# Fetching the attention projection's results as whole tiles, with the conv taps spaced two per cent closer

## The chip, the cores and the metric

The kernel runs on one core of one Trainium2 chip. The metric is the device time of one execution in microseconds, as the median of several runs. The engines are PE (TensorE matmul; PEld its weight load), DVE (VectorE), ACT (ScalarE), POOL (GpSimd) and SP (SyncE), whose queue issues this kernel's DMAs in order.

## The reference: a block with a convolution branch and an attention branch

For x of 2048 tokens by 1024 channels, in float32, the reference computes (cut to what matters)

```python
h = rmsnorm(x, norm_g)
glu_in, cgate, q, k, v, agate, merge = split(h @ w_in)         # 7680 columns
conv = conformer_conv(glu_in)     # a * sigmoid(b); 31-tap causal depthwise conv; layernorm; silu
yc = (conv * silu(cgate)) @ w_conv_out
attn = sliding_window_attention(rope(q), rope(k), v, sinks)    # 16 heads, 4 kv heads, window 128
ya = (attn * silu(agate)) @ w_attn_out
merged = sigmoid(m_c) * yc + sigmoid(m_a) * ya
out = rmsnorm(x + merged @ w_out, final_norm_g)
```

In the kernel's names ma and mc are the two merge gates, before their sigmoid, and mp is the result of the attention projection, ya.

## The kernel before, in words

**Tiling.** Two sweeps s of T = 1024 tokens; each sweep is two halves of TH = 512. Channels are tiles of 128 (KC = 8). Activations lie channels first, so a projection of one channel tile e over one half is 8 chunks of the contraction into one PSUM bank of 128x512. Each product is made of three matmuls on a high and a low part of both operands (`product`), so a half takes 24 matmuls and an item, both halves of one e, 48. `load_w` fetches an item's weights as two raw tiles of 256 KB (L266), casts the high part on ACT (L282) and, in sweep 0, subtracts the low part (L262) and stores it; in sweep 1 the low part is fetched again (L284). Weights have four buffers of each kind and are prefetched one item ahead, `early` the raw part another item ahead.

**Stages of a sweep.** First the projections of the normalised input by w_in, with the attention (scores sc, L808 to L885) worked in between them. Then the 8 items of ya, whose evacuation copies the bank (L1052) and stores it to DRAM as d_mp (L1053). Then the 8 items of yc. Then the output stage o: 16 blocks of 128 tokens by 512 columns, 24 matmuls each (L1204), whose weights wo are fetched (L1147), cast (L1149) and split (L262), into the slots C0 to C7. In ya's time the background work prepares uT, the gated convolution result that yc multiplies.

**The evacuation of yc (`yc_item`, inner function `ev`).** For each half: fetch the gates ma and mc from DRAM (`load_gate`, DMA L599) and take their sigmoids on ACT (L600), fetch mp's half (L1078); on DVE multiply mp by its gate (L1079), multiply the PSUM bank by the other gate (L1080), which frees the bank; add the two on POOL (L1081); cast to the high part of mT on ACT (L343) and subtract the low part on DVE (L262). mT is what the output stage multiplies by. The profile calls the tiles lma, lmc and lmp.

**Buffers.** `t2k` is a ring of five tiles of 128x512 for such short-lived data (L86): gates on their way in and out, squares, and in yc lma, lmc and lmp. `mm_ps` has three PSUM banks for all big projections. `slot` hands out tiles of 128x1024 by tag; a slot that is taken again waits for the last reader of what was in it. The tags C0 to C7 hold the convolution's results cv until uT is made, and later wo; X0 and X2 hold layernorm's mean and the attention's values, both done before yc; C6, C7 and A14 hold GLU blocks in turn, so that the GLU block 7 waits for the last tap on block 5.

**What sets the order.** PE's order is written out by a planner (`Line`): it counts matmul time and, for background work, lets one operation go out after every so many microseconds (`line.every`; CONV_EVERY for the 31 taps of each channel tile's convolution, L532 for the first and L539 for the others, on DVE), while attention steps go out as chains by due time (ATT_EVERY 13.8 us). Evacuations are issued with raised priority. The other engines' rows are ordered by a scheduler. `od` stamps an operation so that stamped operations keep the order in which they were written.

Of the kernel before, what the change touches and what calls it, by code (L numbers as in the profile page):

```python
# [12 lines left out]
F32 = mybir.dt.float32  # L13
# [3 lines left out]
ALU = mybir.AluOpType  # L17
AX = mybir.AxisListType

P = 128  # L20
S = 2048
D = 1024
KC = D // P
T = 1024
NSWEEP = S // T
NB = T // P
TH = 512
# [16 lines left out]
LN_SUB = 2.6  # L44
GLU_AFTER = (0, 6, 12, 16, 19, 22, 25, 28)
ROPE_EVERY = 3.2
CONV_EVERY = 2.5
ATT_EVERY = 13.8
LAT = (19.0, 18.5)
SCORE_GAP = 3.2  # L50
# [6 lines left out]
def hybrid_block(ctx: ExitStack, tc: tile.TileContext, x, xt, par_d, w_in, w_conv, sinks, w_attn, w_out,  # L57
                 fin_g, rope_t, out):
    nc = tc.nc
    pe, act, dve, pool = nc.tensor, nc.scalar, nc.vector, nc.gpsimd  # L60
# [19 lines left out]
    C = [f"c{i}" for i in range(8)]  # L80
    X = [f"x{i}" for i in range(3)]
    WIDE = {"c6", "c7", "a14"}

    def slot(tag, shape, dt, name):
        n = int(np.prod(shape[1:]))
        full = 1024 + P if tag in WIDE else 1024  # L86
        t = slots.tile([P, full], dt, tag=tag, name=name)
        v = t[:, 0:n]
        if len(shape) == 3:
            v = v.rearrange("p (a b) -> p a b", b=shape[2])  # L90
        elif len(shape) == 4:
            v = v.rearrange("p (a b c) -> p a b c", b=shape[2], c=shape[3])
        return v

    def t2k(name, dt=F32):
        return work.tile([P, TH], dt, tag="t2k", name=name, bufs=5)
# [68 lines left out]
    d_mp = dram.tile([NSWEEP * KC, P, T], F32, name="d_mp")  # L165
# [85 lines left out]
    def od(op):  # L251

        tc.stamp_issue_order_token(op.ins, "chain")
        return op
# [9 lines left out]
    def fetch_raw(src, name, kh):  # L264
        raw = stage.tile([P, 4, P], F32, tag="raw", name=f"raw_{name}{kh}")
        od(nc.sync.dma_start(out=raw, in_=src[:, 4 * kh:4 * kh + 4, :]))  # L266
        return raw

    def load_w(src, name, home=None, steps=None, raws=None):

        parts = []
        at = lo_at.setdefault((src.tensor.name, src.offset), len(lo_at))

        def part(kh):
            if home is None:
                raw = raws[kh] if raws else fetch_raw(src, name, kh)
                hi = stage.tile([P, 4, P], F32R, tag="whi", name=f"whi_{name}{kh}")
                lo = stage.tile([P, 4, P], F32R, tag="wlo", name=f"wlo_{name}{kh}")
            else:
                raw, hi, lo = (home[i][:, kh] for i in range(3))  # L280
                od(nc.sync.dma_start(out=raw, in_=src[:, 4 * kh:4 * kh + 4, :]))
            act.copy(hi, raw)  # L282
            if (at, kh) in lo_stored:
                od(nc.sync.dma_start(out=f(lo), in_=d_lo[at, kh]))  # L284
            else:
                split_lo(lo, raw, hi, dve if steps is not None else pool)
            parts.append((hi, lo))

        for kh in range(2):
            if steps is None:  # L290
                part(kh)
            else:
                steps.append(lambda kh=kh: part(kh))

        def keep(kh):
            if (at, kh) not in lo_stored:
                lo_stored.add((at, kh))
                nc.sync.dma_start(out=d_lo[at, kh], in_=f(parts[kh][1]))

        return lambda k: (parts[k // 4][0][:, k % 4, :], parts[k // 4][1][:, k % 4, :]), keep  # L300

    def product(ps, w, r, k, order=(0, 1, 2)):
        parts = ((w[0], r[:, 0, :]), (w[0], r[:, 1, :]), (w[1], r[:, 0, :]))
        for i, (a, b) in enumerate(parts[n] for n in order):
            pe.matmul(out=ps, lhsT=a, rhs=b, start=(k == 0 and i == 0), stop=(k == KC - 1 and i == 2))  # L305

    def small_bank(name):
        return tp_ps.tile([P, 4, P], F32, tag="tp", name=name).rearrange("p a b -> p (a b)")

    def project(src, rhs, name, evac, halves=(0, 1), small=False):  # L310

        got = {}

        def early():
            got["raws"] = [fetch_raw(src, name, kh) for kh in range(2)]

        def prefetch():
            got["w"] = load_w(src, name, raws=got.get("raws"))

        prefetch.early = early  # L320

        def blocks():
            for half in halves:
                if small:
                    ps = small_bank(f"mm_{name}{half}")
                else:
                    ps = mm_ps.tile([P, TH], F32, tag="mm", name=f"mm_{name}{half}")
                for k in range(KC):
                    product(ps, got["w"][0](k), rhs(k, half), k)
                    if k == KC - 1:  # L330
                        with tc.high_priority(offset=PRIO):
                            evac(half, ps)
                    if half == halves[-1] and k % 4 == 3:
                        got["w"][1](k // 4)
                    yield 3 * MM_US

        return prefetch, blocks, (src, name, evac)
# [4 lines left out]
    def put_split(dst, src32, lo_eng):  # L342
        act.copy(dst[:, 0, :], src32)  # L343
        split_lo(dst[:, 1, :], src32, dst[:, 0, :], lo_eng)

    def make_tiles(tags, half, name):
        return [slot(tags[half * 8 + k], [P, 2, TH], F32R, f"{name}{half}_{k}") for k in range(KC)]
# [164 lines left out]
    def program():  # L512
        for s in range(NSWEEP):
            yield from sweep(s)

    def sweep(s):
# [80 lines left out]
        def load_gate(kind, func, e, half):  # L597
            g = t2k(f"l{kind}{s}_{e}_{half}")
            nc.sync.dma_start(out=g, in_=spill[kind][s * KC + e, :, half * TH:(half + 1) * TH])  # L599
            act.activation(out=g, in_=g, func=func)  # L600
            return g
# [293 lines left out]
        def start_attention():  # L895
            line.after(10.0, prepare_attention(), lambda: True)
            for n in range(NKV * NB):
                line.after(22.0 + n * ATT_EVERY, attention(n),
                           lambda n=n: (n > 0 or 0 in qk or 0 in begun) and (n not in soft or ("ag", 2 * (n // NB) + 1) in stored))
            line.every = CONV_EVERY  # L900
            start_tail()
# [75 lines left out]
        aT, uT = [[None] * KC, [None] * KC], []  # L977
# [27 lines left out]
        def start_tail():  # L1005
            line.late.append((line.t, a_chain(), lambda: NKV * NB - 1 in done))
# [61 lines left out]


        mT = []  # L1070

        def yc_item(e):
            def ev(half, ps):
                if not mT:
                    mT.extend(make_tiles(AT, h, f"mT{s}_") for h in range(2))
                ga, g = (load_gate(kind, AF.Sigmoid, e, half) for kind in ("ma", "mc"))
                m = t2k(f"lmp{s}_{e}_{half}")
                nc.sync.dma_start(out=m, in_=d_mp[s * KC + e, :, half * TH:(half + 1) * TH])  # L1078
                dve.tensor_tensor(out=ga, in0=m, in1=ga, op=ALU.mult)  # L1079
                dve.tensor_tensor(out=g, in0=ps, in1=g, op=ALU.mult)  # L1080
                pool.tensor_tensor(out=g, in0=g, in1=ga, op=ALU.add)  # L1081
                put_split(mT[half][e], g, dve)

            return project(w_conv[e], lambda k, half: uT[half][k], f"yc{s}_{e}", ev)

        def linked(item, after):
            def prefetch():
# [3 lines left out]
            return prefetch, item[1]  # L1091

        flat += [ya_item(e, e == 0) for e in range(KC)] + [yc_item(e) for e in range(KC)]
        for item, after in zip(flat, flat[1:]):
            yield linked(item, after)
# [186 lines left out]
```

## Time and profile before

| | |
|---|---|
| median of 3 runs | 2012.25 us (2010.91 to 2016.99) |
| the profiled execution, its own time | 2014.66 us |
| its span | 2013.0 us |
| its mean granted TensorE clock | 0.995 |
| bytes moved | 402.92 MB, mean 200 GB/s |

The span is the stretch from the first to the last recorded instruction; the profiled execution's own time is 1.66 us longer than its span and 2.41 us over the median. All times of the trace are microseconds from the span's start. A row of the waits tells which instruction waited for which, for how long in all, how often, and the longest. In a row of the timeline the figures at the front are start and duration, and the bracket at the end is the engine's idle time before it, with what ended it. For yc, sweep 0 spans 816.20 to 916.58 and sweep 1 1818.00 to 1911.04; ya stands ahead of it, o behind.

### The profile page before, as it was taken

To read this page: it belongs to the slowest core of one execution; us is meant where nothing else is said; L and a number is where in the kernel's file an instruction comes from. 1 tells how busy PE (TensorE), PEld (TensorE's weight loads), DVE (VectorE), ACT (ScalarE), POOL (GpSimd) and SP (SyncE) were. 2 spreads that over 40 slices of the span, in tenths; PEclk is the share of its full clock that TensorE was granted. 3 is DMA by queue.
4 is the path that set the end of the run, shared out by engine and by line. 5 is a ranking of instruction groups with operands and counts; after the bars stand their busy time and mean duration, and the time that the engine had idled before them with its cause. 6 is when DMAs were issued, how large, how long until landed. Compare 5 with 4: busy or idle time off the path is not lost. (4 is left out here: it accounts for less than half of the span.)

```text
span 2013.0 us, 26940 instructions
## 1 busy us (share of the span) xinstructions
PE 1975.2 (98%) x9000; PEld 1637.7 (81%) x9000; DVE 1375.4 (68%) x1937; ACT 1019.6 (51%) x2396; POOL 430.2 (21%) x462
## 2 busy tenths in 40 slices
PE   8999999999999999989999999999999999999998
PEld 6888888888888888867888888888887888888777
DVE  6997688888888646343858657888887875452324
ACT  7322567556555346434623126776655554473322
POOL 0445333333333232341001121111111110001200
PEclk9999999999999999999999999999999999999999
DMA  8557755655666855757546575656565678466632
GB/s 305 189 186 225 240 171 185 198 184 185 193 199 209 283 163 184 234 196 259 209 136 241 167 235 174 188 184 193 187 188 181 211 223 263 156 235 209 224 132 84
DMA packets 296763, 402.92 MB, mean 200 GB/s; under 512 B 23984, under 2 KB 139056, under 8 KB 296624
## 3 DMA queue, kind: packets, MB, share of 16 engines
q1 hardware_dynamic: 296624, 401.20, 61.0%
q8 instruction: 71, 1.16, 0.2%
q14 instruction: 68, 0.56, 0.1%
HBM read 260.59 MB, written 140.51 MB: 199 GB/s over the span
## 5 line engine op out<-in xcount | busy, mean ns | idle before, releaser
L539 DVE SCALAR_TENSOR_TENSOR acc<-glu,par,acc 128x1024 f32<-128x1024 f32 x464 | 595.4, 1283 | 5.1
L1204 PE MATMUL o<-wo,mT 128*128 128x512 f32 x768 | 181.2, 397 | 9.5 <-ACT wo L1149 6.6
L1204 PEld LDWEIGHTS o<-wo,mT 128*128 128x128 f32 x768 | 146.4, 191 | 43.9 <-ACT wo L1149 7.9
L305 PE MATMUL mm_yc<-uT,whi_yc 128*128 128x512 f32 x512 | 160.6, 395 | 12.4 <-DVE lmc L1080 12.4
L305 PE MATMUL mm_cg<-hT,whi_cg 128*128 128x512 f32 x512 | 159.8, 393 | 0.0
L305 PE MATMUL mm_ma<-hT,whi_ma 128*128 128x512 f32 x512 | 159.6, 393 | 0.0
L305 PE MATMUL mm_ag<-hT,whi_ag 128*128 128x512 f32 x512 | 159.4, 392 | 0.0
L305 PE MATMUL mm_mc<-hT,whi_mc 128*128 128x512 f32 x512 | 158.3, 390 | 0.0
L305 PE MATMUL mm_ya<-aT,whi_ya 128*128 128x512 f32 x512 | 157.7, 389 | 0.0
L305 PE MATMUL mm_ga<-hT,whi_ga 128*128 128x512 f32 x448 | 139.5, 392 | 2.2 <-ACT glu L562 2.2
L305 PE MATMUL mm_gb<-hT,whi_gb 128*128 128x512 f32 x448 | 139.2, 392 | 0.0
L851 POOL TENSOR_SCALAR_AFFINE_SELECT pc<-pt 64x512 fp32r<-64x512 f32 x128 | 83.8, 654 | 250.2 <-ACT pt L846 225.8
L305 PEld LDWEIGHTS mm_yc<-uT,whi_yc 128*128 128x128 f32 x512 | 97.2, 191 | 35.0 <-issue 12.8
L872 DVE TENSOR_TENSOR ss<-ov,ss 64x256 f32<-64x256 f32 x128 | 54.0, 422 | 101.5 <-ACT ss L869 94.4
L305 PEld LDWEIGHTS mm_ya<-aT,whi_ya 128*128 128x128 f32 x512 | 96.1, 188 | 20.0
L305 PEld LDWEIGHTS mm_mc<-hT,whi_mc 128*128 128x128 f32 x512 | 95.2, 188 | 18.9
L305 PEld LDWEIGHTS mm_ag<-hT,whi_ag 128*128 128x128 f32 x512 | 94.4, 188 | 17.0
L305 PEld LDWEIGHTS mm_ma<-hT,whi_ma 128*128 128x128 f32 x512 | 94.3, 188 | 16.9
L305 PEld LDWEIGHTS mm_cg<-hT,whi_cg 128*128 128x128 f32 x512 | 94.0, 188 | 16.7
L818 DVE TENSOR_TENSOR ss<-sc,ss 128x192 f32<-128x192 f32 (+2 forms) x256 | 77.7, 345 | 38.8 <-ACT ss L815 37.3
L826 ACT ACTIVATE ss<-ss,st 128x129 f32<-128x129 f32 x256 | 100.0, 394 | 5.9 <-DVE st L823 5.6
L1079 DVE TENSOR_TENSOR lma<-lmp,lma 128x512 f32<-128x512 f32 x32 | 24.4, 763 | 114.5 <-DMA lmp<-d_mp 69.6
(452 smaller groups left out, 4428.9 us busy)
## 6 DMA issues: line engine op xcount, KB each, us to landing
qk<-d_q SPq DMA_DIRECT2D x64, 256.0 KB, 4.3
d_a<-ss SPq DMA_DIRECT2D x64, 256.0 KB, 3.6
aT<-d_a SPq DMA_DIRECT2D x32, 512.0 KB, 6.1
qk<-d_k SPq DMA_DIRECT2D x60, 256.0 KB, 4.5
d_k<-hlk SPq DMA_DIRECT2D x16, 512.0 KB, 4.7
d_q<-hq_c SPq DMA_DIRECT2D x16, 512.0 KB, 4.7
raw_ag<-in_w_in_dram SPq DMA_DIRECT2D x32, 256.0 KB, 4.7
d_ag<-ag SPq DMA_DIRECT2D x32, 256.0 KB, 2.8
```

The lines of the kernel that those rows point to most:

```text
L305: pe.matmul(out=ps, lhsT=a, rhs=b, start=(k == 0 and i == 0), stop=(k == KC - 1 and i == 2))
L539: od(dve.scalar_tensor_tensor(out=to, in0=glu[c][:, j:j + T], scalar=tap(c, j), in1=acc[c], op0=ALU.mult, op1=ALU.add))
L818: od(dve.tensor_tensor(out=part, in0=sc[:, 0, c0:3 * HD], in1=part, op=ALU.add))
L826: od(act.activation(out=ext[:, h, :], in_=ext[:, h, :], func=AF.Exp, bias=ngm[:, h:h + 1], accum_out=den[:, h:h + 1]))
L851: pool.affine_select(out=pc[at], in_=f(pt[0:HD, a]), pattern=[[0, 2 * GQ], [1, HD]], compare_op=ALU.is_ge, fill=0.0, base=0, channel_multi ...
L872: od(dve.tensor_tensor(out=to[r], in0=ovp[rows[r][0], :, r], in1=to[r], op=ALU.add))
L1079: dve.tensor_tensor(out=ga, in0=m, in1=ga, op=ALU.mult)
L1204: pe.matmul(out=ps, lhsT=a[:, c0:c0 + P], rhs=r, start=(k == 0 and i == 0), stop=(k == KC - 1 and i == 2))
```

## The change

The fetch of mp leaves the evacuation. An item's prefetch, which runs one item ahead of its matmuls, now also takes a slot of 128x1024, fetches both halves of mp into it by one DMA of 512 KB, and stamps that DMA so that it keeps its place among the weights' fetches. The slots are X2 and X0 for the first two items and C0 to C5 for the other six. The evacuation reads its half of that tile. The number of taps and of every other operation stays; the taps go out every 2.45 us of planned time in place of 2.5.

```diff
-CONV_EVERY = 2.5
+CONV_EVERY = 2.45
...
         mT = []
+        mp = {}
+        mp_tags = [X[2], X[0]] + C[0:6]
 
         def yc_item(e):
             def ev(half, ps):
...
                 ga, g = (load_gate(kind, AF.Sigmoid, e, half) for kind in ("ma", "mc"))
-                m = t2k(f"lmp{s}_{e}_{half}")
-                nc.sync.dma_start(out=m, in_=d_mp[s * KC + e, :, half * TH:(half + 1) * TH])
-                dve.tensor_tensor(out=ga, in0=m, in1=ga, op=ALU.mult)
+                dve.tensor_tensor(out=ga, in0=mp[e][:, half * TH:(half + 1) * TH], in1=ga, op=ALU.mult)
...
-            return project(w_conv[e], lambda k, half: uT[half][k], f"yc{s}_{e}", ev)
+            prefetch, blocks, _ = project(w_conv[e], lambda k, half: uT[half][k], f"yc{s}_{e}", ev)
+
+            def with_mp():
+                prefetch()
+                mp[e] = slot(mp_tags[e], [P, T], F32, f"mp{s}_{e}")
+                od(nc.sync.dma_start(out=mp[e], in_=d_mp[s * KC + e]))
+
+            with_mp.early = prefetch.early
+            return with_mp, blocks
```

Three places of the rows' order are needed below. In the names, the first figure behind lma, lmc, lmp or mm_yc is e and the second the half, so lma_5_0 is half 10 of the stage and lma_5_1 half 11 (both counted from 0); mT_0_4 is the tile of half 8 and mT_1_4 that of half 9. The last number of a name only tells tiles apart.

The first piece is SP's queue amid yc of sweep 1. Before:

```order
L599 DMA lma_4_0_16956<-d_ma 128x512
L599 DMA lmc_4_0_16959<-d_mc 128x512
L1078 DMA lmp_4_0_16962<-d_mp 128x512
L284 DMA wlo_yc_50_16920<-d_lo 128x512
L284 DMA wlo_yc_51_16924<-d_lo 128x512
L599 DMA lma_4_1_16994<-d_ma 128x512
L266 DMA raw_yc_60_16927<-in_w_conv_out_dram 128x512
L599 DMA lmc_4_1_16997<-d_mc 128x512
L266 DMA raw_yc_61_16929<-in_w_conv_out_dram 128x512
L1078 DMA lmp_4_1_17000<-d_mp 128x512
L599 DMA lma_5_0_17044<-d_ma 128x512
```

The same place after:

```order
L599 DMA lma_4_0_16936<-d_ma 128x512
L599 DMA lmc_4_0_16939<-d_mc 128x512
L599 DMA lma_4_1_16972<-d_ma 128x512
L284 DMA wlo_yc_50_16898<-d_lo 128x512
L284 DMA wlo_yc_51_16902<-d_lo 128x512
L1089 DMA mp_5_16905<-d_mp 128x1024
L599 DMA lmc_4_1_16975<-d_mc 128x512
L266 DMA raw_yc_60_16907<-in_w_conv_out_dram 128x512
L266 DMA raw_yc_61_16909<-in_w_conv_out_dram 128x512
L599 DMA lma_5_0_17022<-d_ma 128x512
```

The two fetches of lmp are gone, one fetch of mp for the next item stands behind that item's low weight parts, and the gate lma_4_1 has moved ahead of them.

The second piece is DVE at the same place. Before:

```order
L1079 TENSOR_TENSOR lma_4_1_16994<-lmp_4_1_17000,lma_4_1_16994 128x512
L262 TENSOR_TENSOR mT_0_4_16592<-lmc_4_0_16959,mT_0_4_16592 128x512
L1079 TENSOR_TENSOR lma_5_0_17044<-lmp_5_0_17050,lma_5_0_17044 128x512
L1080 TENSOR_TENSOR lmc_4_1_16997<-mm_yc_41_16969,lmc_4_1_16997 128x512
L262 TENSOR_TENSOR mT_1_4_16600<-lmc_4_1_16997,mT_1_4_16600 128x512
L1080 TENSOR_TENSOR lmc_5_0_17047<-mm_yc_50_17019,lmc_5_0_17047 128x512
L1079 TENSOR_TENSOR lma_5_1_17082<-lmp_5_1_17088,lma_5_1_17082 128x512
```

After:

```order
L1080 TENSOR_TENSOR lmc_4_0_16939<-mm_yc_40_16911,lmc_4_0_16939 128x512
L262 TENSOR_TENSOR mT_0_4_16580<-lmc_4_0_16939,mT_0_4_16580 128x512
L1079 TENSOR_TENSOR lma_5_0_17022<-mp_5_16905,lma_5_0_17022 128x512
L1080 TENSOR_TENSOR lmc_4_1_16975<-mm_yc_41_16947,lmc_4_1_16975 128x512
L1079 TENSOR_TENSOR lma_5_1_17058<-mp_5_16905,lma_5_1_17058 128x512
L262 TENSOR_TENSOR mT_1_4_16588<-lmc_4_1_16975,mT_1_4_16588 128x512
L1080 TENSOR_TENSOR lmc_5_0_17025<-mm_yc_50_16997,lmc_5_0_17025 128x512
```

Before, L1079 of half 10 stands directly ahead of L1080 of half 9. After, L1079 of half 11 has come ahead of the mT split of half 9: it now runs two halves ahead of its own half's L1080.

The third piece is DVE in sweep 1 where the GLU block 7 is made; cv_5 is the last tap on block 5, acc_6 the first taps on block 6, and the ss rows are pieces of attention steps. Before:

```order
L872 TENSOR_TENSOR ss_2_4_13548<-ov_2_4_13952,ss_2_4_13548 64x256 x2
L873 TENSOR_TENSOR ss_2_4_13548<-ss_2_4_13548,pc_2_4_13754 128x256
L818 TENSOR_TENSOR ss_2_7_13968<-sc_2_7_00_13970,ss_2_7_13968 128x192
L818 TENSOR_TENSOR ss_2_7_13968<-sc_2_7_01_13972,ss_2_7_13968 128x192
L539 SCALAR_TENSOR_TENSOR cv_5_13988<-glu_5_12575,par,acc_5_13224 128x1024
L262 TENSOR_TENSOR ss_2_4_13548<-ss_2_4_13548 128x2x128
L532 TENSOR_SCALAR acc_6_14013<-glu_6_13214,par 128x1024
L566 TENSOR_TENSOR glu_7_13850<-mm_ga_70_13930,glu_7_13850 128x512
```

After:

```order
L539 SCALAR_TENSOR_TENSOR cv_5_13904<-glu_5_12560,par,acc_5_13162 128x1024
L829 RECIPROCAL st_2_6_13865<-st_2_6_13865 128x4
L532 TENSOR_SCALAR acc_6_13933<-glu_6_13201,par 128x1024
L539 SCALAR_TENSOR_TENSOR acc_6_13933<-glu_6_13201,par,acc_6_13933 128x1024
L872 TENSOR_TENSOR ss_2_4_13535<-ov_2_4_13942,ss_2_4_13535 64x256 x2
L873 TENSOR_TENSOR ss_2_4_13535<-ss_2_4_13535,pc_2_4_13740 128x256
L818 TENSOR_TENSOR ss_2_7_13958<-sc_2_7_00_13960,ss_2_7_13958 128x192
L818 TENSOR_TENSOR ss_2_7_13958<-sc_2_7_01_13962,ss_2_7_13958 128x192
L566 TENSOR_TENSOR glu_7_13837<-mm_ga_70_13919,glu_7_13837 128x512
```

The end of block 5 and the start of block 6 have gone ahead of the attention pieces L872 to L818.

## The prediction

> **What bounds the kernel now.** I read the page's head first, then PE's waits, then the stages.
>
> ```profile
> span 2013.0 us, 26940 instructions
> PE 1975.2 (98%) x9000; PEld 1637.7 (81%) x9000; DVE 1375.4 (68%) x1937; ACT 1019.6 (51%) x2396; POOL 430.2 (21%) x462
> ```
>
> PE is busy for 98% of the span, so the change, which leaves the 9000 matmuls as they are, can win only what PE stands idle or runs slowly. The waits of PE (us in total, times, longest) say at what:
>
> ```profile
> PE mm_yc L305 <- DVE lmc L1080: 12.4, 6, 4.0
> PE o L1204 <- ACT wo L1149: 6.6, 3, 4.1
> PE mm_gb L305 <- ACT u_c L380: 5.9, 1, 5.9
> PE mm_ga L305 <- ACT glu L562: 2.2, 1, 2.2
> PE o L1204 <- DVE lmc L1080: 1.8, 1, 1.8
> PE o L1204 <- DVE wo L262: 1.1, 3, 0.6
> PE sc L808 <- DVE ss L818: 0.3, 1, 0.3
> ```
>
> The first row is the convolution's output projection (yc) waiting for a PSUM bank, which L1080 empties. The second, fifth and sixth stand at the start of the output stage (o) that follows. The third is the opening, which the change doesn't touch; the fourth, a projection waiting for the evaluation of a GLU block.
>
> The cost is larger than the waits. The busy time by stage (stretch, length, then PE, PEld, DVE, ACT and POOL, granted clock, DMA share, GB/s) for the attention projection ya, for yc and for o, of sweep 0 and then of sweep 1; the last row is a stretch amid attention:
>
> ```profile
> 728.64:816.20 87.56, 87.56 (x388) 72.45 (x387) 46.32 (x54) 53.91 (x86) 21.97 (x16) 1.00 0.58 193
> 816.20:916.58 100.38, 89.83 (x386) 72.71 (x384) 33.97 (x46) 36.94 (x62) 35.82 (x27) 0.98 0.66 213
> 916.58:1010.50 93.92, 90.97 (x388) 73.89 (x389) 55.36 (x95) 48.81 (x114) 4.21 (x5) 0.98 0.63 225
> 1730.45:1818.00 87.55, 87.55 (x387) 72.45 (x386) 37.12 (x45) 49.07 (x78) 0.00 (x0) 1.00 0.59 198
> 1818.00:1911.04 93.04, 89.35 (x385) 72.87 (x384) 29.99 (x45) 37.00 (x62) 16.76 (x13) 0.98 0.67 225
> 1911.04:2006.40 95.36, 90.66 (x385) 73.43 (x384) 34.85 (x56) 24.09 (x56) 4.36 (x3) 0.96 0.29 111
> 400.00:500.00 100.00, 100.00 (x483) 83.99 (x482) 88.09 (x132) 63.58 (x179) 33.96 (x42) 1.00 0.57 180
> ```
>
> All three stages have 384 matmuls of one shape. Unstalled they take 87.56 us (ya), 5.47 per half of 24, 0.228 per matmul. Yc is over that by 12.82 and 5.49, o by 6.36 and 7.81: **32.5 us** in the four, at a clock below 1.00 each time. The listed waits in them are 21.9 us (rows 1, 2, 5 and 6); the other 10.6 is slow running after a wait:
>
> ```profile
> 877.47 0.70 PE L305 MATMUL mm_yc<-uT,whi_yc 128*128 128x512 f32 x2 [3.98 <-DVE lmc L1080]
> 1898.33 0.70 PE L305 MATMUL mm_yc<-uT,whi_yc 128*128 128x512 f32 x2 [2.82 <-DVE lmc L1080]
> 1921.15 1.52 PE L1204 MATMUL o<-wo,mT 128*128 128x512 f32 x2 [4.08 <-ACT wo L1149]
> ```
> ```profile
> 877.40:882.40 5.00, 4.93 (x15) 3.93 (x16) 1.29 (x2) 1.46 (x3) 2.56 (x2) 0.66 0.73 230
> 1920.00:1930.00 10.00, 8.85 (x27) 6.81 (x28) 2.59 (x4) 1.96 (x4) 1.28 (x1) 0.68 1.02 410
> ```
>
> Behind the 3.98 and the 4.08 the clock is 0.66 and 0.68, and in 5 us 15 matmuls ran where 22 fit.
>
> **Why L1080 is late.** It stands on DVE behind L1079 of the next half (front part, second order piece), and L1079 waits for its third tile:
>
> ```profile
> L1079 DVE TENSOR_TENSOR lma<-lmp,lma x32: 685/693/1692, 826.2 to 1918.0; 128x512 f32<-128x512 f32 x32
>   DMA lmp<-d_mp: 69.6, 24
> DMA to landing us min/median/max: 2.6/3.6/6.3
> ```
>
> 69.6 us of DVE idle in 24 of 32 cases. The load isn't slow, it is issued late: five buffers, three for a half. Two halves in sweep 1 (DVE, one SP issue):
>
> ```profile
> 1860.71 0.69 DVE L262 TENSOR_TENSOR mT<-lmc,mT 128x512 fp32r<-128x512 f32 x1 [2.11 <-ACT mT L343]
> 1861.43 0.32 SPq L1078 DMA_DIRECT2D lmp<-d_mp  x1
> 1865.07 0.69 DVE L1079 TENSOR_TENSOR lma<-lmp,lma 128x512 f32<-128x512 f32 x1 [3.07 <-DMA lmp<-d_mp]
> 1865.68 0.69 DVE L262 TENSOR_TENSOR mT<-lmc,mT 128x512 fp32r<-128x512 f32 x1
> 1870.80 0.69 DVE L1079 TENSOR_TENSOR lma<-lmp,lma 128x512 f32<-128x512 f32 x1 [4.43 <-DMA lmp<-d_mp]
> 1874.20 0.69 DVE L262 TENSOR_TENSOR mT<-lmc,mT 128x512 fp32r<-128x512 f32 x1 [2.11 <-ACT mT L343]
> ```
>
> The split of mT ends at 1861.40, which frees the buffer; the load goes out 0.03 later, lands, and only then does DVE go on. Two halves take 13.49 us here; the same place eight halves apart is
>
> ```profile
> 1847.97 0.69 DVE L262 TENSOR_TENSOR mT<-lmc,mT 128x512 fp32r<-128x512 f32 x1 [2.12 <-ACT mT L343]
> 1900.29 0.69 DVE L262 TENSOR_TENSOR mT<-lmc,mT 128x512 fp32r<-128x512 f32 x1
> ```
>
> 52.32 / 8 = 6.54 us a half against PE's 5.47. Sixteen halves fall 17.1 us behind; the banks beside the one in work let PE run ahead by two halves, 10.9. The 6.2 that is left is of the size of yc's excess (12.82 and 5.49), and the arrears are presented when o wants mT.
>
> **The change, part by part.**
>
> *Whole tiles, loaded ahead.* 32 loads of 256 KB become 16 of 512 KB, the same bytes; SP saves 16 issues of 0.32 us. The nearest row for the new load is an equal size elsewhere (page's DMA issues, last number us to landing):
>
> ```profile
> aT<-d_a SPq DMA_DIRECT2D x32, 512.0 KB, 6.1
> ```
>
> It is issued an item (two halves, 10.9 us) before its first reader, so 6.1 is covered by 4.8; its slot is one whose last reader (statistics or conv output) is done in ya, so it holds up nothing on SP. Cost: nothing; without that cover, issued with its first half as lmp was, it would take the 2.5 more that 6.1 is over lmp's 3.6. On SP the second gate load of an item now stands ahead of the next item's two low weight parts (first order piece), and they wait with it for a buffer: half 9's load for the split of half 6, about 42 us into yc, while half 10, their first reader, starts at 54.7. No cost.
>
> *The loop that remains.* The view of the tile lma has the gate's sigmoid and the landing:
>
> ```profile
> L600 ACT ACTIVATE lma<-lma x32: 627/632/635, 823.6 to 1916.5; 128x512 f32<-128x512 f32 x32
> DMA to landing us min/median/max: 2.5/3.1/6.5
> ```
>
> Two tiles of five a half: the gate's load of half h+3 waits for the mT split of half h. After the change L1079 of half h+2 stands between L1080 and the mT split of half h (second order piece), so each split waits for the load that the split before it released: 0.69 (split) + 3.1 (landing) + 0.63 (L600) + 0.61 (L1079, start to next start: 1865.07 to 1865.68) = **5.03 us**, under 5.47. The other way round, L1080, POOL's add, cast and split, was in the trace of before 1870.80 to 1874.20 with L1079 ahead of it, 3.4, shorter. So yc should not stall. It breaks even at a landing of 3.54; and since 10.9 us of arrears fit into the banks, a landing of 4.2 (16 × 0.68) costs yc nothing yet.
>
> What is late next is o's start. Half 14's bank is full 5.47 before yc ends, its chain takes 3.4, and o wants that tile (k = 7) 21 matmuls, 4.8 us, into its first block: 6.9 us of slack, or 0.43 a half, a loop of 5.90 and a landing of 3.97. The last weight was late for another reason:
>
> ```profile
> 1914.33 0.32 SPq L1078 DMA_DIRECT2D lmp<-d_mp  x1
> 1914.70 0.42 SPq L1147 DMA_DIRECT2D rawo<-in_w_out_dram  x1
> 1920.48 0.62 ACT L1149 CAST wo<-rawo 128x512 fp32r<-128x512 f32 x1 [2.03 <-DMA rawo<-in_w_out_dram]
> ```
>
> It stood on SP behind the last lmp, which waited for a buffer until after yc's end (1911.04), and landed with 410 GB/s in flight. Without lmp nothing ahead of it waits. The new constraint, wo's slots C0 to C5 free only after the last read of mp 2 to 7, ends with L1079 of half 15, which now runs two halves ahead of L1080: no later than yc's end. So o's 6.36 and 7.81 go too, bounded by 0 and 14.2.
>
> *Taps at 2.45.* Same 31 x 8 operations a sweep, 2% closer, on DVE:
>
> ```profile
> L539 DVE SCALAR_TENSOR_TENSOR acc<-glu,par,acc 128x1024 f32<-128x1024 f32 x464 | 595.4, 1283 | 5.1
> 1529.25 1.27 DVE L539 SCALAR_TENSOR_TENSOR cv<-glu,par,acc 128x1024 f32<-128x1024 f32 x1
> ```
>
> The single row is the last tap of channel block 5; its end at 1530.52 frees the slot for the next GLU block, and the 2.2 in the fourth row of PE's waits follows from it. It is some 155 taps into the line, so 155 × 0.05 = 7.7 us earlier, and the third order piece has it ahead of the attention step's pieces: the 2.2 goes. DVE's share in attention rises by about a point from 88.09, while PE has 0.3 us of waits on it there. Cost between 0 and what rival 4 says; taken as 0.
>
> **Sum.** 32.5 + 2.2 = 34.7 us can go. I keep 2.0 of it as residual, between 0 and 6.2 (one sweep's arrears as now), near the low end since the loop is 0.44 under PE's. The profiled run took 2014.66, so 2014.66 − 32.7 = 1982.0; it lies 2.4 above the median 2012.25, so the median is **1979.5**, 1.6% faster.
>
> [...]
>
> **Rivals.**
>
> 1. *The gate loop takes lmp's place.* If beside the 512 KB loads a gate tile lands after 4.3 (between the median 3.1 and the longest 6.5), the loop is 6.23: 16 × 0.76 = 12.2 behind, 1.3 more than the banks hold, and of their 10.9 another 4.0 over o's slack of 6.9; with slow matmuls behind both 6 us a sweep, 1979.5 + 12 = 1991.5. For: the DMA share is 0.66 already, and the same bytes now come in fewer, longer loads. Against: 3.1 is a median under that share. Chance 0.14. [...]
> 2. *o's start stays late* for the weights' own reasons (cast, split, the 410 GB/s burst): 14.2 stays, 1979.5 + 14.2 − 2.0 = 1991.7. Against: that transfer's issue is tied to lmp by the rows. Chance 0.08.
> 3. *No effect in yc and o*: L1079 waits at its old time because the gate tiles, not lmp, are what the buffers hold back, so the loop stays 6.54. Only 2.2 goes: 2010. Against: 24 of 32 waits end with lmp. Chance 0.05.
> 4. *Slower.* Taps moved ahead of the attention's pieces on DVE: each delays the score chain by 1.28, and the third order piece shows two taps gone past L872 and L818. If it happened at all 64 attention steps and came through to PE, 64 × 1.28 = 82: 2012.25 − 34.7 + 82 = 2060. It decides from 34.7 + 6 = 41 us, 0.64 a step, half of the steps. Against: PE's waits for DVE there are 0.3 us, and DVE is idle 11.9% of it, 1.6 us in each 13.8 of a step. Chance 0.05.
>
> **How the numbers follow.** The forecast has 0.68 (1979.5). A run of this kernel can tell 0.3%, 6 us, from no change. Forecast and rivals 1 and 2 are faster: 0.90; rival 3 is the same, 0.05; rival 4 slower, 0.05. The range goes from 1975 (no residual, 1977.5; the lowest run's 1.3 under its median; 1.2 of small waits) to 1996 (rivals 1 and 2 near 1992, plus 4 for the spread upward, as the highest run's 2016.99 has 4.7). It leaves out rivals 3 and 4 and the edges.
>
> **What would show it.** Right: yc and o of 87.6 to 89 us in both sweeps at a clock of 1.00; no row of mm_yc on lmc in PE's waits, none of mm_ga on glu; L1079 waiting for no tile of d_mp; o's first weights cast before yc's end; attention's stretch near 89 of DVE. Wrong: mm_yc still waiting, with L1079 now idle on lma's load over 3.5 us (rival 1) or at its old times (3); o waiting on wo (2); waits of sc or the probabilities' matmuls on DVE in the attention stage (4).

## The result, and the profile after

The changed kernel takes **1981.73 us** (median of 4 runs, 1980.19 to 1983.12) against 2012.75 of the kernel before, measured beside it: a ratio of 0.9843, 95% interval 0.9825 to 0.986. The forecast was 1979.5, with a range of 1975 to 1996. The profiled execution took 1982.04 us with a span of 1980.3. Of the executions reported further down, one of the four of e8_after_bank took 4031.6 us, at a clock of 1.00 and about twice as long as the other three; it is left out of that run's figure, and what made it so long is not known.

The page's head and the waits of PE (us in total, times, longest), after:

```profile
span 1980.3 us, 26884 instructions
PE 1965.2 (99%) x9000; PEld 1634.1 (83%) x9000; DVE 1382.8 (70%) x1937; ACT 1018.8 (51%) x2396; POOL 430.8 (22%) x462
```
```profile
PE mm_gb L305 <- ACT u_c L380: 5.6, 1, 5.6
PE o L1212 <- ACT mT L343: 1.2, 1, 1.2
PE sc L808 <- DVE ss L818: 1.1, 4, 0.3
```

The rows of mm_yc on lmc (12.4), of o on wo (6.6), of mm_ga on glu (2.2), of o on lmc (1.8) and of o on the splits of wo (1.1) are gone. New are 1.2 us of o on mT, and 0.8 more of the scores. L1204 of before is L1212 now.

Busy time by stage after: ya, yc and o of sweep 0, then of sweep 1.

```profile
729.32:816.87 87.55, 87.55 (x387) 72.48 (x386) 40.56 (x45) 49.20 (x77) 21.65 (x17) 1.00 0.64 216
816.87:903.91 87.04, 87.04 (x385) 72.11 (x384) 35.80 (x49) 38.20 (x65) 35.39 (x27) 1.00 0.72 233
903.91:993.85 89.94, 88.69 (x390) 72.62 (x388) 53.73 (x92) 46.62 (x110) 2.92 (x4) 1.00 0.63 225
1711.99:1799.55 87.56, 87.56 (x388) 72.48 (x387) 36.72 (x44) 48.53 (x76) 0.00 (x0) 1.00 0.59 198
1799.55:1886.59 87.04, 87.04 (x386) 72.10 (x385) 36.92 (x53) 41.37 (x70) 19.34 (x15) 1.00 0.79 270
1886.59:1973.80 87.21, 87.20 (x385) 71.91 (x383) 29.32 (x49) 19.49 (x48) 1.28 (x1) 1.00 0.21 86
```

Yc has neither a wait nor a slow stretch in either sweep. Against the rows of before, yc gives 13.34 and 6.00, o 3.98 and 8.15. The projections ahead of ya, in both kernels (before, then after):

```profile
0.00:728.64 728.64, 721.55 (x3342) 599.94 (x3343) 593.73 (x832) 399.25 (x993) 254.40 (x269) 1.00 0.64 209
1010.50:1730.45 719.95, 717.73 (x3348) 599.98 (x3346) 541.82 (x762) 368.81 (x945) 92.64 (x130) 1.00 0.62 197
```
```profile
0.00:729.32 729.32, 722.28 (x3342) 600.19 (x3343) 605.70 (x841) 404.07 (x1002) 257.17 (x269) 1.00 0.64 208
993.85:1711.99 718.14, 717.79 (x3347) 600.18 (x3346) 541.91 (x762) 369.58 (x946) 93.01 (x130) 1.00 0.62 198
```

Sweep 0 pays 0.68 for the closer taps (with 12 us more of DVE's work done ahead of ya), sweep 1 gains 1.81. With 0.10 at the end, −13.34 − 6.00 − 3.98 − 8.15 + 0.68 − 1.81 − 0.10 = −32.70, the whole difference of the spans, 2013.0 − 1980.3.

In yc, DVE's rows of sweep 0 (mT splits, the one at 868.23 left out, and the L1079 ahead of the third), and of sweep 1 (L1080):

```profile
851.96 0.69 DVE L262 TENSOR_TENSOR mT<-lmc,mT 128x512 fp32r<-128x512 f32 x1
857.02 1.36 DVE L262 TENSOR_TENSOR mT<-lmc,mT 128x512 fp32r<-128x512 f32 x1 [0.34 <-ACT mT L343]
862.50 0.69 DVE L1079 TENSOR_TENSOR lma<-mp,lma 128x512 f32<-128x512 f32 x1 [3.52 <-ACT lma L600]
863.11 0.68 DVE L262 TENSOR_TENSOR mT<-lmc,mT 128x512 fp32r<-128x512 f32 x1
874.47 0.69 DVE L262 TENSOR_TENSOR mT<-lmc,mT 128x512 fp32r<-128x512 f32 x1
```
```profile
1832.38 0.69 DVE L1080 TENSOR_TENSOR lmc<-mm_yc,lmc 128x512 f32<-128x512 f32 x1 [1.26 <-PE mm_yc L305]
1859.59 0.69 DVE L1080 TENSOR_TENSOR lmc<-mm_yc,lmc 128x512 f32<-128x512 f32 x1 [1.92 <-PE mm_yc L305]
```

In sweep 1 five halves take 27.21 us, 5.44 each, and L1080 waits for PE: the evacuation has become the faster of the two. In sweep 0 two halves take 11.15 (851.96 to 863.11) and 11.36, 5.6 each, and L1079 waits for the gate's sigmoid, hence for the gate's load: there the loop is still a little slower than PE's 5.44, which the banks absorb. At the end of yc of sweep 0 another thing comes on top:

```profile
898.46 0.68 DVE L1080 TENSOR_TENSOR lmc<-mm_yc,lmc 128x512 f32<-128x512 f32 x1
907.32 0.69 DVE L1080 TENSOR_TENSOR lmc<-mm_yc,lmc 128x512 f32<-128x512 f32 x1
```

Between these two evacuations, of halves 13 and 14, lie 8.86 us in place of 5.6. DVE's order has four splits of o's weights between them, the last of which (906.71) waits 1.34 us for ACT's cast of a weight that had just landed (the cast, at 906.05, had itself waited 1.41 us for it). O's one wait, of 1.2 us at 910.12, is for the mT that half 14 makes.

### The profile page after: what moved, and what is told of

It is laid out like the page before. It is cut to its first block, busy times and chain, and to the rows that moved or that the text cites. A ratio compares the mean times of both kernels' runs of the same rounds, so it can differ in the third digit from the quotient of the medians.

```text
span 1980.3 us, 26884 instructions
## 1 busy us (share of the span) xinstructions
PE 1965.2 (99%) x9000; PEld 1634.1 (83%) x9000; DVE 1382.8 (70%) x1937; ACT 1018.8 (51%) x2396; POOL 430.8 (22%) x462
## 4 chain that ended last, share of the span: by engine, by line
PE 53%; DMA 2%; DVE 1%; ACT 1%; issue 1%; POOL 0%; SPq 0%; POOLq 0%; ACTq 0%
PE o L1212 9%; PE mm_cg L305 4%; PE mm_ma L305 4%; PE mm_gb L305 4%; PE mm_mc L305 4%; PE mm_ya L305 4%; PE mm_yc L305 4%; PE mm_ag L305 4%; PE mm_ga L305 4%; PE mm_q_a L305 2%; PE mm_q_b L305 2%; PE mm_v L305 1%; PE ov L862 1%; PE sc L808 1%; DMA lma<-d_ma 1%; PE tpp L838 1%
## 5 line engine op out<-in xcount | busy, mean ns | idle before, releaser
L1212 PE MATMUL o<-wo,mT 128*128 128x512 f32 x768 | 175.4, 390 | 1.2 <-ACT mT L343 1.2
L1212 PEld LDWEIGHTS o<-wo,mT 128*128 128x128 f32 x768 | 144.0, 188 | 32.1 <-ACT mT L343 1.7
L872 DVE TENSOR_TENSOR ss<-ov,ss 64x256 f32<-64x256 f32 x128 | 54.0, 422 | 95.0 <-ACT ss L869 87.2
L818 DVE TENSOR_TENSOR ss<-sc,ss 128x192 f32<-128x192 f32 (+2 forms) x256 | 77.5, 344 | 37.0 <-ACT ss L815 35.4
L305 PE MATMUL mm_cg<-hT,wlo_cg 128*128 128x512 f32 x256 | 100.2, 391 | 0.0
```

The source lines that it names most:

```text
L818: od(dve.tensor_tensor(out=part, in0=sc[:, 0, c0:3 * HD], in1=part, op=ALU.add))
L872: od(dve.tensor_tensor(out=to[r], in0=ovp[rows[r][0], :, r], in1=to[r], op=ALU.add))
L1212: pe.matmul(out=ps, lhsT=a[:, c0:c0 + P], rhs=r, start=(k == 0 and i == 0), stop=(k == KC - 1 and i == 2))
```

## The experiments

**Theory A**, as first held: the third tile's fetch is released late because three tiles a half go round in five buffers, and the bank's evacuation stands behind it. Its rivals: **B**, the count of buffers alone; **C**, the number and size of the transfers; **D**, the closer taps.

### e1_taps_only and e2_tiles_only: the two halves of the change

The first is the kernel before with `CONV_EVERY = 2.45`, the second the changed kernel with `CONV_EVERY = 2.5`.

> The kernel before with the taps at 2.45 and lmp left as it was. Theory A (the third tile's fetch, released late and standing ahead of the bank's evacuation on DVE, makes the 30 us): only the GLU wait of 2.2 us goes, and at most 1 us is paid in attention: 2010.5 us, PE's wait of mm_yc on lmc stays at 9 to 13 us. Rival D (the closer taps carry a good part, by an earlier layernorm and so an earlier start of yc's loads): under 2004 us, mm_yc's wait halved.

> The changed kernel with the taps back at 2.5. Theory A: 1983 us (1981.7 plus about 1.5: the GLU wait of 2.2 comes back, 0.7 of the attention's cost goes), yc at 87.0 us in both sweeps without a wait. Rival D: over 1990 us.

Measured: taps alone 2010.28 us, ratio 0.9977 (0.9965 to 0.999); tiles alone 1985.68, ratio 0.9859 (0.9843 to 0.9875). Rival D falls: with the taps alone, PE still waits in yc.

```profile
PE mm_yc L305 <- DVE lmc L1080: 9.4, 5, 3.6
```

Of the 31.0 us the tiles bring some 27, the taps 2 by themselves and 4.0 on top of the tiles. The 4.0 (4.8 between the two profiled executions) is more than the GLU wait. Where the rest is, the waits and the stage rows of the tiles alone show (yc, then o, sweep 0):

```profile
PE mm_ga L305 <- ACT glu L562: 2.2, 1, 2.2
PE o L1212 <- ACT wo L1157: 1.5, 1, 1.5
PE o L1212 <- ACT mT L343: 1.0, 1, 1.0
```
```profile
815.91:902.95 87.04, 87.04 (x386) 72.11 (x384) 34.09 (x47) 37.27 (x64) 36.53 (x28) 1.00 0.72 241
902.95:995.21 92.26, 89.49 (x390) 72.53 (x388) 56.06 (x95) 48.37 (x113) 3.44 (x5) 1.00 0.64 230
```

O of sweep 0 takes 92.26 there, 89.94 with the taps. The last split of uT and the first L1079 behind it, of the tiles alone and then of the changed kernel:

```profile
815.72 0.69 DVE L262 TENSOR_TENSOR uT<-lcg,uT 128x512 fp32r<-128x512 f32 x1 [0.69 <-ACT uT L343]
826.32 0.69 DVE L1079 TENSOR_TENSOR lma<-mp,lma 128x512 f32<-128x512 f32 x1 [9.91 <-ACT lma L600]
```
```profile
803.21 0.69 DVE L262 TENSOR_TENSOR uT<-lcg,uT 128x512 fp32r<-128x512 f32 x1 [0.69 <-ACT uT L343]
824.26 0.69 DVE L1079 TENSOR_TENSOR lma<-mp,lma 128x512 f32<-128x512 f32 x1 [20.36 <-DMA lmc<-d_mc]
```

248 taps by 0.05 is 12.4 us, and the last uT is 12.5 earlier. Yc's evacuation then begins 10.4 us after yc's start in the one and 7.4 in the other. As sweep 0's loop gains nothing on PE, 2.3 of those 3 us are still there at the end: L1080 of half 14 starts 5.71 us into o with the tiles alone and 3.41 with the taps. The projections of sweep 1 give the other part: 721.54 us with the tiles alone, 718.14 with the taps, 3.4 less for a wait of 2.2, because with the tiles alone the clock in the 5 us behind that wait is 0.66 (15 matmuls). In the kernel before, behind the same wait, it is 1.00 (22 matmuls). Against both, the projections of sweep 0 take 0.96 more with the closer taps.

### e3_six_buffers and e4_bank_first: buffers or order

The kernel before with one number changed, and with two rows exchanged:

```diff
-        return work.tile([P, TH], dt, tag="t2k", name=name, bufs=5)
+        return work.tile([P, TH], dt, tag="t2k", name=name, bufs=6)
```
```diff
-                dve.tensor_tensor(out=ga, in0=m, in1=ga, op=ALU.mult)
-                dve.tensor_tensor(out=g, in0=ps, in1=g, op=ALU.mult)
+                od(dve.tensor_tensor(out=g, in0=ps, in1=g, op=ALU.mult))
+                od(dve.tensor_tensor(out=ga, in0=m, in1=ga, op=ALU.mult))
```

> The kernel before with six buffers of 128x512 in place of five; lmp is still fetched half by half, 32 loads of 256 KB, taps at 2.5. Theory A: the fetch no longer waits for the split of the half before last but for the one before that; a pass over two halves is then about 8.1 us, 4.1 a half against PE's 5.4, so mm_yc's wait goes and the time is 1983 to 1988 us. Rival C (it is the number and size of the transfers that counts): mm_yc's wait stays at 9 us or more, over 2005 us.

> The kernel before, five buffers and 32 loads of lmp, taps at 2.5, but with the evacuation of the bank written and kept ahead of the product with lmp on DVE, half by half. Theory A: the fetch is released as late as before, but the bank no longer waits behind it. In series a half then costs DVE 0.68 + 0.69, POOL 1.29, ACT 0.62, DVE 0.69, with the waits between about 4.2 us, and the next fetch (3.7) fits beside it: no wait of mm_yc, 1983 to 1990 us. Rival B (three tiles in five buffers are too few whatever the order, a loop of 6.5 us): the waits stay, over 2005 us.

Measured: six buffers 2006.23, ratio 0.9963 (0.9946 to 0.9979); bank first 1993.85, ratio 0.99 (0.9885 to 0.9915). **Both missed their ranges, the first by 18 us, and theory A in its first form falls.** With six buffers the time is in rival C's range, but its wait isn't there: PE's wait in yc is halved, from 12.4 to 5.7. What six buffers did, DVE and SP in yc of sweep 1:

```profile
1854.16 0.69 DVE L1080 TENSOR_TENSOR lmc<-mm_yc,lmc 128x512 f32<-128x512 f32 x1
1856.96 0.69 DVE L262 TENSOR_TENSOR mT<-lmc,mT 128x512 fp32r<-128x512 f32 x1 [2.12 <-ACT mT L343]
1860.65 0.69 DVE L1079 TENSOR_TENSOR lma<-lmp,lma 128x512 f32<-128x512 f32 x1 [2.99 <-DMA lmp<-d_mp]
1866.66 0.69 DVE L1080 TENSOR_TENSOR lmc<-mm_yc,lmc 128x512 f32<-128x512 f32 x1
```
```profile
1856.30 0.32 SPq L1078 DMA_DIRECT2D lmp<-d_mp  x1
```

Two halves, 1854.16 to 1866.66, take 12.5 us: 6.25 a half, hardly less than 6.54. With six, the load goes out when POOL's add of this half ends (L1080 ends at 1854.85, the add takes 1.3, the load goes out at 1856.30; 22 of SP's waits at L1078, 28.6 us, end with that add), and L1079 of a later half, which stands ahead of the next L1080, waits for it. A load in the loop was exchanged for another. With five buffers and the bank first, no evacuation of the bank stands behind a load of a later half:

```profile
PE mm_yc L305 <- DVE lmc L1079: 1.5, 2, 1.2
PE o L1204 <- ACT wo L1149: 2.9, 3, 1.9
```
```profile
815.67:905.25 89.58, 87.84 (x385) 71.67 (x383) 31.08 (x45) 36.47 (x62) 34.77 (x27) 1.00 0.70 231
905.25:1001.88 96.63, 92.86 (x388) 74.86 (x389) 57.20 (x97) 50.00 (x116) 4.17 (x5) 0.96 0.65 228
1811.01:1898.05 87.04, 87.04 (x386) 72.07 (x384) 32.46 (x50) 38.33 (x65) 18.09 (x14) 1.00 0.77 256
```

(L1079 is the row on the bank here.) Yc is at 89.58 and 87.04 with three tiles in five buffers, so rival B falls. O of sweep 0 is worse than before, 96.63, while o of sweep 1 takes 87.25. In sweep 0 the last two loads of lmp go out at 906.47 and 912.98, after yc's end, and stand on SP among those of o's weights; what that costs was not measured by itself. What holds, theory A': *a load is released by one half's evacuation, and DVE's order puts its reader ahead of the next half's; so every half pays a landing.* The change works since it takes the late load out and leaves a gate's load with a loop of 5.4 to 5.6.

### e5_half_loads and e6_own_item: size and lead of the load

```diff
-                od(nc.sync.dma_start(out=mp[e], in_=d_mp[s * KC + e]))
+                for half in range(2):
+                    hs = slice(half * TH, (half + 1) * TH)
+                    od(nc.sync.dma_start(out=mp[e][:, hs], in_=d_mp[s * KC + e, :, hs]))
```
```diff
+
+            def with_fetch():
                 od(nc.sync.dma_start(out=mp[e], in_=d_mp[s * KC + e]))
+                yield from blocks()
 
             with_mp.early = prefetch.early
-            return with_mp, blocks
+            return with_mp, with_fetch
```

> The changed kernel, but each item's mp comes in two loads of 256 KB (one for each half) into the same slot at the same place, 32 loads as before. Theory A (what counts is that the load is out of the evacuation's loop): as the changed kernel, 1980 to 1984 us. Rival C (size and number of transfers count): half or more of the 30 us comes back, over 1995 us.

> The changed kernel with the load of mp stamped at the start of its own item in place of an item ahead (same slot, one load of 512 KB). Theory A: a landing of 3.6 to 6.1 still ends about when the item's first half is done (5.4), and nothing in the load waits for a buffer: 1982 to 1987 us, no wait of mm_yc over 1 us. Rival (the lead of an item is what hides it): each item's first half waits 1 to 3 us, yc 95 us or more, over 1992 us.

Measured: half loads 1982.96, ratio 0.9851 (0.9837 to 0.9866), the changed kernel's time within the interval, so rival C falls: number and size of the loads show no effect here. Own item 1996.65, ratio 0.9912 (0.9893 to 0.9931): a miss. About half of the gain is gone with the lead. DVE and the stage rows (yc of both sweeps; the profiled execution, 2001.76, is the longest of the four):

```profile
1868.52 1.29 DVE L1079 TENSOR_TENSOR lma<-mp,lma 128x512 f32<-128x512 f32 x2 [3.82 <-DMA mp<-d_mp]
1871.65 0.69 DVE L262 TENSOR_TENSOR mT<-lmc,mT 128x512 fp32r<-128x512 f32 x1 [1.84 <-ACT mT L343]
```
```profile
818.10:907.00 88.90, 87.64 (x386) 71.84 (x384) 33.24 (x46) 36.78 (x62) 35.01 (x27) 1.00 0.70 232
1807.00:1899.86 92.86, 89.69 (x386) 72.93 (x384) 30.08 (x46) 37.72 (x62) 19.88 (x14) 0.98 0.67 225
```

L1079 of both halves waits 3.82 us for mp, and the mT split stands behind them on DVE: a late load in front of the evacuation once more, now once an item. O pays as well (its waits on wo come to 4.8). The lead of an item is part of what works.

### e7_after_six and e11_gate_whole: more of the same

The changed kernel with `bufs=6`; and with the gate ma loaded whole, an item ahead (cut; so that ma finds free slots, mp's tiles move to other slots too):

```diff
+        ma = {}
...
+                ga = ma[e][:, hs]
+                act.activation(out=ga, in_=ga, func=AF.Sigmoid)
...
+                ma[e] = slot(ma_tags[e], [P, T], F32, f"ma{s}_{e}")
+                od(nc.sync.dma_start(out=ma[e], in_=spill["ma"][s * KC + e]))
```

> The changed kernel with six buffers of 128x512. Theory A: what is left of the excess, 2 us at the start of o in sweep 0, comes from yc's first gate loads, which wait for buffers that ya's last stores hold; with a sixth they go out earlier and the wait of o on mT (1.2 us) goes: 1979 to 1981 us. Rival: the loads are released by other instructions then, as in the run with six buffers, and a new wait appears: 1984 us or more.

> The changed kernel with the gate ma of an item treated as mp is: one load of 512 KB an item ahead into free slots, its sigmoid still taken half by half. In sweep 0 the changed kernel's splits follow each other every 5.6 us, released by the gate's load, a little over PE's 5.44. Theory A: that loop is gone, o of sweep 0 loses its wait on mT (1.2 us): 1979 to 1981 us. Rival C (whole tiles compete with the weights' loads): waits on weights appear, 1983 us or more.

Measured: 1988.96, ratio 0.9881 (0.9867 to 0.9896), and 1984.73, ratio 0.9862 (0.9842 to 0.9882). Both missed; neither beats the change. The second is in its rival's range, but with no wait on weights. With six buffers DVE has, in yc of sweep 0,

```profile
863.57 0.69 DVE L1079 TENSOR_TENSOR lma<-mp,lma 128x512 f32<-128x512 f32 x1 [1.50 <-ACT lma L600]
864.18 0.68 DVE L1080 TENSOR_TENSOR lmc<-mm_yc,lmc 128x512 f32<-128x512 f32 x1
875.64 0.69 DVE L1079 TENSOR_TENSOR lma<-mp,lma 128x512 f32<-128x512 f32 x1 [1.52 <-ACT lma L600]
```

12.07 us for two halves, 6.0 each: again the gate's load is released by the add of the half before its reader, and yc of sweep 0 takes 92.65. This is the rival that was named, and A' once more. With the gate whole, o of sweep 0 does lose its wait (88.06 us), as expected, but yc waits for the bank instead (L1085 in place of L1080, L1084 of L1079):

```profile
PE mm_yc L305 <- DVE lmc L1085: 2.8, 2, 1.8
```
```profile
871.38 1.29 DVE L1084 TENSOR_TENSOR ma<-mp,ma 128x512 f32<-128x512 f32 x2 [2.57 <-ACT ma L1082]
```

The products of both halves of the next item stand together ahead of the bank and wait 2.57 us for that item's sigmoid (L1082, 870.72), which had itself waited 2.11 us for the gate's landing, 6.4 us after the load went out at 864.34: a load ahead of the evacuation again. Yc of sweep 0 takes 90.85 there, 3.8 longer, so that o starts later. That o lost its wait doesn't show, therefore, that the gate's loop had made it.

### e8_after_bank, e10_bank_x and e9_x_slots: the slots that mp shares with wo

The first exchanges L1079 and L1080 in the changed kernel as above; the second also, and the third only, has

```diff
-        mp_tags = [X[2], X[0]] + C[0:6]
+        mp_tags = [X[2], X[0], X[1]] * 2 + [X[2], X[0]]
```

> The changed kernel with the evacuation of the bank kept ahead of the product with mp on DVE, half by half. Theory A in its second form (the loop closes through a load only because L1079 stands ahead of L1080): no bank waits behind any load, the series of a half is 4.2 us, yc 87.0 in both sweeps, 1980 to 1983 us. If instead the lead of L1079 was of use, the series of add, cast and split now comes later and o's start waits 2 to 4 us a sweep: 1985 to 1990 us.

> The run with the bank ahead of mp, with mp's tiles in X2, X0 and X1 in turn. There the sixth weight of o in sweep 0 was cast only after the product with mp of half 15, because they share C5, and PE waited 5.1 us. If that sharing is the cause, 4 to 6 us come back: 1988 to 1991 us. If DVE's order at the end of yc is (the last products stand behind the splits of weights that land late), nothing does: 1993 to 1996 us.

> The changed kernel with mp's tiles in X2, X0 and X1 in turn, so that no slot of wo waits for a reader of mp. The prediction's step (that wait costs nothing while L1079 runs two halves ahead): as the changed kernel, 1980 to 1984 us, o of sweep 0 at 89.9. Rival (the slots do hold up o's first weights): o of sweep 0 under 89 us, 1978 to 1980 us.

Measured: bank first 1993.56 (three executions), ratio 0.9904 (0.9887 to 0.9921), later than both of its ranges; with the X slots 1982.37, 0.9856 (0.9829 to 0.9882); the change with the X slots 1983.57, 0.9857 (0.9837 to 0.9876). With the bank first yc is at 87.04 twice, and o of sweep 0 takes 99.83. PE, and ACT's cast of the sixth weight:

```profile
915.17 0.80 PE L1212 MATMUL o<-wo,mT 128*128 128x512 f32 x1 [5.11 <-ACT wo L1157]
```
```profile
914.50 0.62 ACT L1157 CAST wo<-rawo 128x512 fp32r<-128x512 f32 x1 [1.96 <-DVE lma L1080]
```

The cast waits for the product with mp of half 15 (L1080 here), which shares C5. With mp in the X slots the same stage is

```profile
904.94:994.34 89.40, 88.63 (x389) 72.67 (x388) 54.85 (x93) 46.63 (x110) 2.92 (x4) 1.00 0.62 220
```

10.4 us less, more than expected. So the shared slots are a real constraint. In the changed kernel, where L1079 runs ahead, they cost nothing: with the X slots (e9) the time is no shorter, and o of sweep 0 takes 91.24.

### e12_taps_24: closer still

The changed kernel with `CONV_EVERY = 2.4`.

> The changed kernel with the taps at 2.4. Theory A: the GLU wait is already gone and the first gate loads of yc no longer wait for uT but for ya's stores, so nothing more is won, and the waits of scores on DVE go up from 1.1 to about 2 us: 1981 to 1984 us. Rival D (closer taps go on winning as they did from 2.5 to 2.45): 1977 to 1979 us.

Measured: 1983.79, ratio 0.9857 (0.9837 to 0.9876): no further gain, as expected. The scores' waits on DVE, 0.6 and 0.5, stayed at 1.1 in all, not 2. Still closer taps weren't tried.

## Why the prediction was right, and where its steps were off

- **The bound and the cause.** Right: PE's excess in yc and o was what was at stake, yc's was made by the load that L1079 waited for, and all of it went. The cause was put too simply, as three tiles in five buffers: e3 shows that a sixth buffer leaves 6.25 a half, e4 that order alone takes yc's waits from 12.4 to 1.5. Number of buffers and DVE's order make the loop together. O's part went with the change too, but its causes were not taken apart: with the order alone o of sweep 1 is cured (87.25) and o of sweep 0 is not (96.63).
- **The loop that remains.** Forecast 5.03 a half, under PE's 5.47; measured 5.6 in sweep 0, over it, and PE's own 5.44 in sweep 1. The landing was sized right: between 851.96 and 863.11 the two gate loads take 2.65 and 3.43 us from their issue to their sigmoids, 6.1 against the sum's 6.2. What the sum left out, 1.1 us in two halves, is that in the middle of sweep 0 every other mT split starts 0.4 later, since it waits for ACT's cast, and lasts 1.36 in place of 0.69. POOL splits a weight at those times (L262, 856.54 to 857.83, for one); in sweep 1, where it splits none, no mT split is longer than 0.69. Whether the one makes the other longer was not tested.
- **The wait of o on mT.** The first L1080 of sweep 0 runs 2.6 us after its bank is full (824.87 against 816.87 + 5.44), which the prediction left out, and the one of half 13 runs 5.4 after. At 5.6 a half, half 14's would have come at 904.06, and with a chain of 3.4 its mT 1.4 us before PE asked for it at 908.87. It came 3.3 us later, behind the splits of o's weights on DVE, and o waited 1.2. That is rival 2's mechanism, the weights' own reasons, at 1.2 us in place of 14.2. Rival 1's, gate tiles that land after 4.3 us, is not there: their median is 3.4.
- **The lead and C0 to C5.** Both steps held for the kernel as changed. The price named for a missing lead, 2.5 us where the load isn't covered, left out that DVE's order hands it on: e6 lost half of the gain. The condition named for the slots, that L1079 runs ahead, is what they hang on: without it they cost 11 us (e8 against e10).
- **O's start, and the stage without stalls.** Forecast that both 6.36 and 7.81 go; gone are 3.98 and 8.15. The prediction took every stage for 384 matmuls. Sweep 0's o also holds four of the next sweep's norm (L375), 4 × 0.228 = 0.9, which the sum took for excess. The other way round, ya holds two more (lnvar) in each sweep, so that the stall-free stage is 87.04 and not 87.56, and each of the four excesses was 0.5 larger than written. Counted so, 33.6 us were at stake and not 32.5, and the 2.0 that are left in o of sweep 0 are 89.94 against 87.95.
- **The taps.** Forecast 2.2 for the GLU wait and nothing else. The wait went; beside it the closer taps bring the end of uT, and so the start of yc's evacuation in sweep 0, forward, which the prediction didn't see and which is worth the 2.3 us of o between e2 and the change. Their cost, taken as 0, was 0.68 in sweep 0, and sweep 1 gained 1.81 and not 2.2. Rival 4's mechanism is there too, at 0.8 us of scores' waits in place of 82.
- **The sum.** Forecast 1982.0 for the profiled execution, 1982.04 measured. That this fits to 0.04 is luck. Yc gave 1.0 us more than written, o 2.0 less, the taps and the end 1.0 less, and the 2.0 kept as residual happened to cover the difference. The reason given for its size, a loop 0.44 under PE's, did not hold in sweep 0. The median is 2.2 over the forecast since the offset between it and the profiled execution, taken over from before as 2.4, was 0.3 here.
- **Waits against slow running.** Right: with the 21.9 + 2.2 of waits the 10.6 of slow running went too, and the clock is 1.00 in all six stages. Not every wait is followed by slow running, though: behind one of 2.14 us the clock was 1.00 (last section).

## What to carry to other kernels

In a loop on an engine whose written order counts, as DVE's did here (two rows exchanged took yc's waits from 12.4 us to 1.5, e4), ask for each load which instruction frees its buffer and what stands behind its reader: where a later step's reader is ordered ahead of this step's evacuation, every step pays a landing (here 6.54 us a half against PE's 5.47), and another buffer may only move the release to another instruction of the same loop, as it did here twice (e3, 6.25 a half, and e7, 6.0). Take the load out of the loop by giving it a home of its own and a lead of a whole item, and count as cost what then waits for that home (11 us, e8 against e10). And price a stall with the slow running that may stand behind it (a clock of 0.66 in the 5 us behind a wait of 3.98), from the stage's length against a stage without stalls that has the same number of matmuls, counted.

## What the runs showed of the hardware that was not expected

The clock was 0.66 also behind a wait of 1.85 us, much shorter than those of 3.98 and 4.08, and 1.00 behind others. One and the same wait shows both: in sweep 1 PE stands idle for 2.23 us until the GLU block is evaluated (L562), both in the kernel before and with the tiles alone. In the 5 us behind it the clock is 1.00 with 22 matmuls in the one (from 1531.20) and 0.66 with 15 in the other (from 1515.91), and the projections of sweep 1, in which it stands, take 719.95 us in the one and 721.54 in the other. Two more rows: a wait and the 5 us behind it, with the taps alone and then with the changed kernel and six buffers:

```profile
1894.74 0.47 PE L305 MATMUL mm_yc<-uT,whi_yc 128*128 128x512 f32 x1 [1.85 <-DVE lmc L1080]
```
```profile
1894.74:1899.74 5.00, 5.00 (x15) 4.01 (x16) 3.01 (x3) 2.16 (x5) 2.56 (x2) 0.66 0.57 188
```
```profile
903.47 0.73 PE L305 MATMUL mm_yc<-uT,whi_yc 128*128 128x512 f32 x2 [2.14 <-DVE lmc L1080]
```
```profile
903.47:908.47 5.00, 5.00 (x22) 4.16 (x23) 0.91 (x2) 1.54 (x4) 1.29 (x1) 1.00 0.47 151
```

After 1.85 us the clock is 0.66 and 15 matmuls run where 22 fit; after 2.14 it is 1.00 and all 22 run. In these rows the length of the wait alone doesn't tell which it will be. What decides between a drop and none was not tested.
